# A fifth group of seven products in the values' second unit, and softmax's last scale on ScalarE

## The chip, the cores and the metric

The kernel runs on one core of one Trainium2 chip. The metric is the time of one execution on the device in microseconds, as the median of several runs. Everything is computed in float32 accuracy; there is one launch.

## The reference

One decoder layer on 256 tokens of width 2048. A combined projection feeds a state-space group of heads and an attention group; both outputs are concatenated, projected back and added to the input; a squared-ReLU MLP of width 8192 follows. RMSNorm stands before and after each half. What the change touches is the values' projection and the attention's softmax:

```python
proj = jnp.einsum('bsd,de->bse', u, w_in)
z, xbc, dt_raw, q, k, v = jnp.split(proj, IN_SPLITS, axis=-1)
...
s = jnp.where(mask[None, :, None], s, -jnp.inf)
m = jnp.max(s, axis=-1, keepdims=True)
p = jnp.exp(s - m)
den = jnp.sum(p, axis=-1)
o = jnp.einsum('bnqhk,bnkhd->bnqhd', p, vb) / jnp.swapaxes(den, 2, 3)[..., None]
```

There are three such branches (dilations 1, 4 and 16), weighted by their softmax denominators. The kernel folds them into one softmax, with the logarithm of the number of branches that see a key as the mask; the rows are divided by the sum before they are multiplied with the values.

## The kernel before

**Products in three.** TensorE multiplies in a reduced form of float32. So every factor is split in two: `hi`, the rounded value, written by ScalarE (L147), and `lo`, the rest, written by VectorE (L148). Each product is three matmuls: hi by hi, hi by lo, lo by hi. Weights are fetched as `raw` tiles of 256 x 512 (two blocks of 128 rows), split, and used as the moving side; the activations, split once, are the standing side. Tokens are two blocks of 128.

**Plain groups and groups of seven.** Most large projections are made in units: two blocks of 512 columns, walked over k, where one k is two 128-row blocks of weights. For one k there are two token blocks, two row blocks and two column blocks: eight products, 24 matmuls (`row_tile`, L331 to L333). In the form of Winograd's variant of Strassen's scheme (`seven`, L418 to L420) seven products of sums of blocks, 21 matmuls, do the same. They need sums of the weights' blocks (`add_in_line`, L252, three of 128x512 on VectorE), which are then split too: 3.5 tiles of 128x1024 instead of 2. They also need sums of the activations' blocks (`sums_of_acts`, L377 to L380 and a split of 128x512), which are kept per k in `room["sums"]` and used by every unit on the same activations. The sum of two row blocks of weights is made by GpSimd's DMA, which adds one block to the other in DRAM (`next_pair`, L279 and L280), four groups of seven ahead; SyncE then fetches that sum and the second block (L156 and L157) in place of one transfer (L161).

**What sets the order.** A scheduler orders each engine's instructions by the program's order and by priorities; splits, sums and combinations have a high one (`AHEAD`). `split_in_line` and `add_in_line` keep weights in one line. There are four raw tiles (`RAWS`) and five hi and lo tiles (`BUFS`). Which k come in which order, and which by seven, is a table per unit, the calls of `plan` (from L434 on); the same calls give the order of GpSimd's pairs.

**The stage.** Queries and keys of 4 heads at a time are computed with features in the partitions (`queries`, L485 and L488, blocks of `cT`, a ring of five tiles of 128 x 4 x 256) or by units with transposes behind. Around the change the program runs: queries of the last block; the values' second unit (`two_values(2, ...)`, with `room["sums"]` holding the sums of four k: 1, 3, 5, 6); keys of the last block; then the output projection. `own_places` takes two tiles of the ring as scratch for the unit. Meanwhile the heads' attention waits in a queue, from which each tile of a projection pumps a step; a unit drains it before its first group of seven. A step is: scores (L907, L908) for two heads; mask, row minimum of the negated scores (L915, VectorE), exponential with the row sum (L917, ScalarE), reciprocal (L919) and scale (L921, both VectorE); then transposes of the scaled rows (L929, TensorE) and their copies (L933, ScalarE); then the products with the values (L938, L939) and their split.

Of the kernel before, what the change touches and what calls it, by code (L numbers as in the profile page):

```python
# [11 lines left out]
F32R = mybir.dt.float32r  # L12
BF16 = mybir.dt.bfloat16
AF = mybir.ActivationFunctionType
ALU = mybir.AluOpType

P = 128
S = 256
# [21 lines left out]
KB = 2  # L40
# [13 lines left out]
V_SEVENS = (1, 3, 5, 6)  # L54
# [23 lines left out]
def hymba_layer(ctx: ExitStack, tc: tile.TileContext, x, norm_mix_pre, w_in, conv_w, conv_b, dt_bias, a_log,  # L78
                d_skip, ssm_norm_w, w_out, norm_mix_post, norm_mlp_pre, w_up, w_down, norm_mlp_post,
                consts, out):  # L80
    nc = tc.nc
# [31 lines left out]
    def part(k):  # L113
        if k < NK:
            return sh, sl, k
        i, r = divmod(k - NK, NK // 2)
        return (*att[i], r)
# [14 lines left out]
    def bank():  # L132
        return pacc.tile([P, NB], F32, name="acc")

    def psmall():
        return psm.tile([P, NB], F32, name="ps")
# [7 lines left out]
    def split(hi, lo, src, scale=None):  # L144

        if scale is None:
            return (nc.scalar.activation(hi, src, AF.Copy),  # L147
                    nc.vector.tensor_tensor(lo, src, hi.bitcast(F32), op=ALU.subtract))  # L148
        return (nc.scalar.activation(hi, src, AF.Copy, scale=scale),
                nc.vector.scalar_tensor_tensor(lo, src, scale, hi.bitcast(F32), op0=ALU.mult, op1=ALU.subtract))  # L150
# [27 lines left out]
    room = {}  # L178
# [77 lines left out]
    w_z, w_v, w_ups, w_downs = w_in[:, COL_Z:], w_in[:, COL_V:], [w_up[:, hf * 4096:] for hf in range(2)], [w_down, w_down[4096:]]  # L256
    orders = {}

    def order_of(ks, by_seven):
        return [(k, k in by_seven) for k in ks]  # L260

    def blocks_of(n):
        return n if isinstance(n, tuple) else (n * NB, (n + 1) * NB)

    def plan(name, src, n, order, by_seven):

        orders[name, n] = order_of(order, by_seven)
        pairs.extend((src, blocks_of(n), k) for k in order if k in by_seven)
# [167 lines left out]
    plan("qk", w_in, qk_blocks[1], (0, 2, 1, 4, 3, 5, 6), QK_SEVENS)  # L436
    plan("v", w_v, 0, range(7), V_SEVENS)
    plan("qk", w_in, qk_blocks[2], (0, 2, 1, 3, 4, 5, 6), QK_SEVENS)
    plan("v", w_v, 2, (0, 2, 1, 3, 4, 5, 6), V_SEVENS)
    plan("out", w_out, 0, (5, 7, 6, 9, 8, 11, 10, 13, 12), (6, 8, 9, 10, 12))  # L440
    plan("out", w_out, 2, (0, 6, 1, 9, 2, 12, 4, 3, 8, 5, 10, 7), (6, 9, 12, 4, 8, 10, 7))
    for hf in range(2):
# [8 lines left out]
    def unit(src, n, order, last, acc, more, combine, lag=0, at_end=(None, None), first=True, ending=None,  # L451
             ready=None, halves=None):


        cols = blocks_of(n)
        sevens = [k for k, by_seven in order if by_seven]
        for i, (k, by_seven) in enumerate(order):
            if i + 1 < len(order) and order[i + 1][1]:
                sums_of_acts(order[i + 1][0])
            if by_seven:  # L460
                if k == sevens[0]:
                    drain()
                    if ready:
                        ready()
                seven(src, *cols, k, acc, more, k == sevens[0], k == sevens[-1])
            else:
                for b in range(2):
                    row_tiles(src, cols[b], [k], acc[b::2], room["acts"], first and i == 0, False,
                              fetch=fetch_next)
            if k == sevens[-1]:  # L470
                combine(more)
        for b in range(2):
            if b and ending:
                ended.append(ending(cols[b], last, acc))
            else:
                row_tiles(src, cols[b], last, acc[b::2], room["acts"], False, True, lag if b else 0, at_end[b],
                          fetch=fetch_last if b else fetch_next, halves=halves if b else None)
# [173 lines left out]
    mp = mid.enter_context(tc.tile_pool(name="mp", bufs=1))  # L651
# [77 lines left out]
    def conv_block(c0, ft0, acc=None):  # L729

        first = acc
        acc = acc or gemm_features(w_in, c0)
        dst = mp.tile([P, 4, S], F32, name="cT", bufs=5)
        for b in range(2):
            added(dst[:, 2 * b:2 * b + 2], acc[2 * b:2 * b + 2])
        if first:
            waiting.append(first_conv(dst, ft0))
        else:
            conv(dst, ft0)
        return dst  # L740
# [28 lines left out]
    def own_places(tiles):  # L769

        own, total = tiles
        room["own"] = deque(own[:, t] for t in range(NT))
        room["sum"] = total
# [111 lines left out]
    for hb in range(2):  # L885
# [3 lines left out]
        cT = conv_block(COL_C + hb * NB, 24 + 4 * hb)  # L889
# [10 lines left out]
    def attention(ap, h, qT, kT, v):  # L900

        spans = ((slice(0, P), m0), (slice(P, 3 * P), m1))
        pair = []
        with tc.issue_after(product[0].ins), tc.issue_after(product[1].ins):
            for j in range(2):
                s = psmall()
                nc.tensor.matmul(s[:, 0:P], qT[:, j, 0:P], kT[:, j, 0:P], start=True, stop=True)  # L907
                nc.tensor.matmul(s[:, P:3 * P], qT[:, j, P:], kT[:, j], start=True, stop=True)  # L908
                pair.append(s)
        for j, s in enumerate(pair):  # L910
            sm = ap.tile([P, 3 * P], F32, name="sm", bufs=4)
            mx = ap.tile([P, 2], F32, name="mx", bufs=4)
            den = ap.tile([P, 2], F32, name="den", bufs=4)
            for t, (cs, mk) in enumerate(spans):
                nc.vector.tensor_tensor_reduce(sm[:, cs], s[:, cs], mk, op0=ALU.add, op1=ALU.min, scale=-1.0,  # L915
                                               scalar=3.0e38, accum_out=mx[:, t:t + 1])
                nc.scalar.activation(sm[:, cs], sm[:, cs], AF.Exp, bias=mx[:, t:t + 1], scale=-1.0,  # L917
                                     accum_out=den[:, t:t + 1])
            nc.vector.reciprocal(den, den)  # L919
            for t, (cs, mk) in enumerate(spans):  # L920
                nc.vector.tensor_scalar(sm[:, cs], sm[:, cs], den[:, t:t + 1], None, op0=ALU.mult)  # L921
            pair[j] = sm
        yield
        turned = []
        with tc.issue_after(product[0].ins), tc.issue_after(product[1].ins):
            for sm in pair:
                p = psmall()
                for b in range(3):
                    nc.tensor.transpose(p[:, b * P:(b + 1) * P], sm[:, b * P:(b + 1) * P], ident)  # L929
                turned.append(p)  # L930
        for j, p in enumerate(turned):
            pair[j] = ap.tile([P, 3 * P], F32, name="pT", bufs=4)
            nc.scalar.activation(pair[j], p[:, :3 * P], AF.Copy)  # L933
        yield
        o = psmall().rearrange("p (j s) -> p j s", j=2)
        with tc.issue_after(product[0].ins), tc.issue_after(product[1].ins):
            for j, pT in enumerate(pair):
                nc.tensor.matmul(o[:, j], v[:, 0, j], pT[:, :S], start=True, stop=False, skip_group_check=True)  # L938
                nc.tensor.matmul(o[:, j, P:], v[:, 1, j], pT[:, S:], start=False, stop=True, skip_group_check=True)  # L939
        d_h, d_l, i = part(NK + h)  # L940
        split(d_h[:, i:i + 2], d_l[:, i:i + 2], o)
# [56 lines left out]
    def two_values(vb, acc, more):  # L998

        values = []  # L1000

        def ready():
            values[:] = [mp.tile([P, NT, NB], F32, name="tk", bufs=3) for _ in range(2)]
            if not more:
                more.extend(f() for f in (psmall, bank, psmall, bank))

        def end(b):
            def at_end(t, a):
                with tc.high_priority(offset=AHEAD):
                    v = values[b][:, t]  # L1010
                    nc.vector.tensor_tensor(v, a, v, op=ALU.subtract if b else ALU.add)
                    nc.scalar.activation(v, v, AF.Copy, scale=rstd[:, t:t + 1])
            return at_end

        unit(w_v, vb, orders["v", vb], (7,), acc, more,
             lambda x: combine_new([[v[:, t] for t in range(NT)] for v in values], x), 0, (end(0), end(1)),
             ready=ready)
        return values
# [34 lines left out]
    heads((0, *qk[0], vs[0]), (1, *qk[1], vs[1]))  # L1053
    q3 = queries(COL_Q + 3 * NB, rbq, (1, 1, 0, 2, 1, 2, 2, 2))
    own_places([mp.tile([P, 4, S], F32, name="cT", bufs=5).rearrange("p (k f) s -> p k (f s)", k=KB) for _ in range(2)])
    vs += two_values(2, [bank() for _ in range(2 * NT)], [])
    heads((2, *qk[2], vs[2]))
    qk.append((q3, queries(COL_K + 3 * NB, rbc, (0, 0, 1, 1, 1, 1, 2, 2))))
# [498 lines left out]
```

## Time and profile before

| | before |
|---|---|
| runs | 1452.44, 1452.65, 1452.96 us |
| median | 1452.65 us |
| span of the profiled execution | 1451.4 us |
| TensorE busy | 1442.4 us, 99% |
| VectorE busy | 1300.4 us, 90% |
| ScalarE busy | 947.1 us, 65% |
| GpSimd busy | 162.3 us, 11% |
| mean granted clock | 0.999 |

The span is the time from the first to the last instruction of one profiled execution; what the runs take beside it is outside the program's instructions. Rows of a timeline give start, length, engine, line, operation and tiles; a bracket gives the idle time of the engine just before and what ended it. Rows that group instructions give the count, the busy time in us, the mean in ns, and behind the second bar the idle time before them. Matmuls overlap in the pipeline, so their starts, not their lengths, tell what one costs.

### The profile page before, as it was taken

The numbers are of one execution on the slowest core, as the hardware profiler recorded it, in microseconds if no ns is written. First come the engines' busy times: TensorE is split into PE (matmuls) and PEld (weight loads), VectorE is DVE, ScalarE is ACT, GpSimd is POOL, SyncE is SP. The second block draws the span as 40 slices with busy tenths as digits, with TensorE's granted clock in tenths as the row PEclk, the third lists the DMA queues.
The fourth block names the chain that finished last, engine by engine and source line by source line (L and its number), as shares of the span: only waits on it lengthen the run. The fifth ranks groups of instructions, "written<-read, shape, count | busy, mean of one in ns | idle before, by whom it ended". The sixth has DMA issues, their size and how long they took to land.

```text
span 1451.4 us, 20394 instructions
## 1 busy us (share of the span) xinstructions
PE 1442.4 (99%) x7042; PEld 1214.7 (84%) x7042; DVE 1300.4 (90%) x1881; ACT 947.1 (65%) x1351; POOL 162.3 (11%) x244
## 2 busy tenths in 40 slices
PE   9999999999999999999999999999999999999998
PEld 8888888888888888888888888888888888888886
DVE  7788888988999788689988999999889999999998
ACT  7577669665666666556657677656465776766664
POOL 0201110131111000010100011010111110101000
PEclk9999999999999999999999999999999999999999
DMA  8977656756898658588976798688888888788854
GB/s 267 272 219 222 189 175 187 239 170 195 231 253 248 196 127 244 173 270 257 280 225 217 210 311 240 203 221 251 249 255 279 255 245 247 210 293 265 248 179 160
DMA packets 172359, 332.97 MB, mean 229 GB/s; under 512 B 16048, under 2 KB 18976, under 8 KB 172256
## 3 DMA queue, kind: packets, MB, share of 16 engines
q1 hardware_dynamic: 144736, 272.37, 58.1%
q0 software_dynamic: 19648, 45.63, 15.7%
q10 hardware_dynamic: 7872, 13.68, 2.8%
q8 instruction: 55, 0.90, 0.3%
q14 instruction: 48, 0.39, 0.1%
HBM read 327.39 MB, written 49.84 MB: 260 GB/s over the span
## 4 chain that ended last, share of the span: by engine, by line
PE 76%; ACT 1%; DVE 1%; DMA 0%; issue 0%; ACTq 0%
PE acc L331 10%; PE acc L333 10%; PE acc L332 10%; PE acc L418 7%; PE acc L419 7%; PE acc L420 7%; PE acc L485 4%; PE ps L331 3%; PE ps L332 3%; PE ps L333 3%; PE ps L418 2%; PE ps L419 2%; PE ps L420 2%; PE acc L488 2%; PE acc L1463 1%; PE ps L938 0%
## 5 line engine op out<-in xcount | busy, mean ns | idle before, releaser
L148 DVE TENSOR_TENSOR lo<-raw,hi 128x1024 fp32r<-128x1024 f32 (+1 forms) x387 | 470.1, 1220 | 79.1 <-ACT hi L147 76.3
L147 ACT ACTIVATE hi<-raw 128x1024 fp32r<-128x1024 f32 (+1 forms) x387 | 404.2, 1050 | 204.2 <-PE acc L333 71.4
L485 PE MATMUL acc<-ua,hi 128*128 128x512 f32 x520 | 141.2, 401 | 0.1
L147 ACT ACTIVATE hi<-e 128x1024 fp32r<-128x1024 f32 x66 | 70.2, 1063 | 68.5 <-DVE e L252 62.7
L485 PEld LDWEIGHTS acc<-ua,hi 128*128 128x128 f32 x520 | 91.3, 189 | 14.2 <-ACT hi L147 0.2
L331 PE MATMUL acc<-hi,ua 128*128 128x512 f32 x228 | 90.6, 397 | 0.0
L332 PE MATMUL acc<-lo,ua 128*128 128x512 f32 x228 | 89.3, 392 | 0.0
L333 PE MATMUL acc<-hi,ua 128*128 128x512 f32 x228 | 89.2, 391 | 0.0
L331 PE MATMUL acc<-hi,sh 128*128 128x512 f32 x220 | 86.9, 395 | 0.0
L333 PE MATMUL acc<-hi,sl 128*128 128x512 f32 x220 | 85.8, 390 | 0.0
L332 PE MATMUL acc<-lo,sh 128*128 128x512 f32 x220 | 85.7, 390 | 0.0
L488 PEld LDWEIGHTS acc<-ua,lo 128*128 128x128 f32 x520 | 76.5, 190 | 8.9
L148 DVE TENSOR_TENSOR lo<-e,hi 128x1024 fp32r<-128x1024 f32 x66 | 80.5, 1220 | 0.0
L488 PE MATMUL acc<-ua,lo 128*128 128x256 f32 x520 | 78.8, 282 | 0.0
L419 PE MATMUL acc<-lo,ah 128*128 128x512 f32 x180 | 70.1, 390 | 0.0
L420 PE MATMUL acc<-hi,al 128*128 128x512 f32 x180 | 70.1, 390 | 0.0
L418 PE MATMUL acc<-hi,ah 128*128 128x512 f32 x180 | 70.1, 390 | 0.0
L485 PE MATMUL acc<-uc,hi 128*128 128x512 f32 x208 | 61.4, 405 | 0.0
L148 DVE TENSOR_TENSOR lo<-ha,hi 128x1024 fp32r<-128x1024 f32 x43 | 52.5, 1221 | 6.0 <-ACT hi L147 5.8
L147 ACT ACTIVATE hi<-ha 128x1024 fp32r<-128x1024 f32 x43 | 45.2, 1057 | 19.4 <-PE acc L333 12.4
L147 ACT ACTIVATE hi<-r 128x512 fp32r<-128x512 f32 x66 | 41.5, 629 | 20.8 <-PE acc L333 8.8
L418 PE MATMUL acc<-hi,ua 128*128 128x512 f32 x137 | 53.7, 392 | 0.0
(572 smaller groups left out, 3722.3 us busy)
## 6 DMA issues: line engine op xcount, KB each, us to landing
raw<-in_w_in_dram SPq DMA_DIRECT2D x154, 512.0 KB, 4.5
raw<-in_w_down_dram SPq DMA_DIRECT2D x69, 512.0 KB, 5.7
raw<-in_w_up_dram SPq DMA_DIRECT2D x65, 512.0 KB, 4.8
raw<-in_w_out_dram SPq DMA_DIRECT2D x38, 512.0 KB, 5.1
raw<-pair SPq DMA_DIRECT2D x57, 256.0 KB, 4.3
pair<-in_w_up_dram POOLq DMA_DIRECT2D x56, 256.0 KB, 5.4
pair<-in_w_down_dram POOLq DMA_DIRECT2D x52, 256.0 KB, 6.3
pair<-in_w_in_dram POOLq DMA_DIRECT2D x42, 256.0 KB, 5.5
```

The costliest lines, as they stand in the source:

```text
L147: return (nc.scalar.activation(hi, src, AF.Copy), nc.vector.tensor_tensor(lo, src, hi.bitcast(F32), op=ALU.subtract))
L148: nc.vector.tensor_tensor(lo, src, hi.bitcast(F32), op=ALU.subtract))
L331: nc.tensor.matmul(dst[:, cs], a_h[:, r, ts], hi[:, j, cs], start=begin and j == 0, stop=False)
L332: nc.tensor.matmul(dst[:, cs], a_h[:, r, ts], lo[:, j, cs], start=False, stop=False)
L333: product[t] = nc.tensor.matmul(dst[:, cs], a_l[:, r, ts], hi[:, j, cs], start=False, stop=end and j == KB - 1)
L418: nc.tensor.matmul(dst, a_h, hi[:, j], start=own and first, stop=False)
L419: nc.tensor.matmul(dst, a_h, lo[:, j], start=False, stop=False)
L420: nc.tensor.matmul(dst, a_l, hi[:, j], start=False, stop=own and last)
L485: nc.tensor.matmul(acc[f], hi[:, j, f * P:(f + 1) * P], u(k0 + j), start=k0 + j == 0, stop=False, skip_group_check=True)
L488: nc.tensor.matmul(acc[f][:, 0], lo[:, j, f * P:(f + 1) * P], u(k0 + j)[:, 0], start=False, stop=k0 + j == NK - 1, skip_group_check=True)
L1463: nc.tensor.transpose(p[:, f * P:(f + 1) * P], r[:, f * P:(f + 1) * P], ident)
```

## The change

The values' second unit takes k = 4 by seven products too: its table of sevens is written out as (1, 3, 4, 5, 6), where it was (1, 3, 5, 6), in the same order of k. The sums of k = 4 get a tile of the ring `cT` of their own, taken just before the unit; the keys' last block therefore takes the next tile of the ring. The last scale of the softmax, one instruction per head and token block, is an activation (a copy with a scale per partition) on ScalarE instead of a multiplication on VectorE.

```diff
-    plan("v", w_v, 2, (0, 2, 1, 3, 4, 5, 6), V_SEVENS)
+    plan("v", w_v, 2, (0, 2, 1, 3, 4, 5, 6), (1, 3, 4, 5, 6))
...
             nc.vector.reciprocal(den, den)
             for t, (cs, mk) in enumerate(spans):
-                nc.vector.tensor_scalar(sm[:, cs], sm[:, cs], den[:, t:t + 1], None, op0=ALU.mult)
+                nc.scalar.activation(sm[:, cs], sm[:, cs], AF.Copy, scale=den[:, t:t + 1])
             pair[j] = sm
...
     own_places([mp.tile([P, 4, S], F32, name="cT", bufs=5).rearrange("p (k f) s -> p k (f s)", k=KB) for _ in range(2)])
+    fifth = mp.tile([P, 4, S], F32R, name="cT", bufs=5)
+    room["sums"] += [fifth[:, i:i + KB] for i in (0, KB)]
     vs += two_values(2, [bank() for _ in range(2 * NT)], [])
```

## The prediction

> **What bounds the kernel now.** I read the page's busy shares and its chain first, then the engines' busy time in stretches of 25 us, then TensorE's and VectorE's timelines in the values' second unit.
>
> ```profile
> span 1451.4 us, 20394 instructions
> PE 1442.4 (99%) x7042; PEld 1214.7 (84%) x7042; DVE 1300.4 (90%) x1881; ACT 947.1 (65%) x1351; POOL 162.3 (11%) x244
> PE 76%; ACT 1%; DVE 1%; DMA 0%; issue 0%; ACTq 0%
> 500.00:525.00 25.00, 25.00 (x141) 21.42 (x140) 21.10 (x72) 17.53 (x49) 2.71 (x4) 1.00 0.54 127
> 525.00:550.00 25.00, 25.00 (x118) 20.83 (x117) 20.12 (x24) 15.11 (x18) 1.89 (x3) 1.00 0.59 170
> ```
>
> TensorE is never seen idle around the change (25.00 of 25), and the chain that ends last is TensorE's. So a matmul less is a gain, and anything that makes TensorE wait is a loss. VectorE has about 5 of 25 us to spare here, ScalarE 8 to 10. The profiled span is 1451.4 us; the timed runs' median is 1452.65, so 1.25 us lie around the span. The sum below is made on the span, and 1.25 is added at the end.
>
> How long a matmul really holds TensorE is read from starts, since neighbours overlap. The unit's fourth group (k = 4), in the plain form, and the two groups of seven after it:
>
> ```profile
> 540.71 0.39 PE L331 MATMUL acc<-hi,ua 128*128 128x512 f32 x1
> 546.15 0.39 PE L418 MATMUL ps<-hi,ub 128*128 128x512 f32 x1
> 550.91 0.39 PE L418 MATMUL ps<-hi,uc 128*128 128x512 f32 x1
> 555.67 0.39 PE L331 MATMUL acc<-hi,uc 128*128 128x512 f32 x1
> ```
>
> 24 matmuls take 546.15 - 540.71 = 5.44 us; 21 take 4.76 us, twice. One costs 0.227 us, not the 0.39 of its own row.
>
> VectorE over the same groups (columns: start, length, and in brackets the idle time before, with what ended it):
>
> ```profile
> 525.89 0.69 DVE L148 TENSOR_TENSOR lo<-cT,hi 128x512 fp32r<-128x512 f32 x1 [1.12 <-ACT hi L147]
> ...
> 529.71 1.23 DVE L148 TENSOR_TENSOR lo<-raw,hi 128x1024 fp32r<-128x1024 f32 x1 [1.79 <-ACT hi L147]
> ...
> 534.34 1.23 DVE L148 TENSOR_TENSOR lo<-cT,hi 128x1024 fp32r<-128x1024 f32 x1 [1.60 <-ACT hi L147]
> ...
> 537.30 2.58 DVE L148 TENSOR_TENSOR lo<-raw,hi 128x1024 fp32r<-128x1024 f32 x2
> 539.80 0.68 DVE L252 TENSOR_TENSOR cT<-raw 128x512 f32<-128x512 f32 x1
> 540.52 0.69 DVE L252 TENSOR_TENSOR cT<-cT,raw 128x512 f32<-128x512 f32 x1
> 541.12 1.22 DVE L148 TENSOR_TENSOR lo<-raw,hi 128x1024 fp32r<-128x1024 f32 x1
> 542.26 0.69 DVE L252 TENSOR_TENSOR cT<-cT,raw 128x512 f32<-128x512 f32 x1
> 542.86 1.22 DVE L148 TENSOR_TENSOR lo<-cT,hi 128x1024 fp32r<-128x1024 f32 x1
> 544.00 1.22 DVE L148 TENSOR_TENSOR lo<-raw,hi 128x1024 fp32r<-128x1024 f32 x1
> 545.13 0.69 DVE L148 TENSOR_TENSOR lo<-cT,hi 128x512 fp32r<-128x512 f32 x1
> 545.73 0.69 DVE L252 TENSOR_TENSOR cT<-raw 128x512 f32<-128x512 f32 x1
> ...
> 547.50 1.23 DVE L148 TENSOR_TENSOR lo<-raw,hi 128x1024 fp32r<-128x1024 f32 x1 [0.35 <-ACT hi L147]
> ```
>
> The rows 539.80 to 545.73 are one whole group of seven (k = 5): 5.93 us on VectorE, against 4.76 us on TensorE. The plain group (537.30 to 539.80) is 2.50 against 5.44. So VectorE falls behind by 1.17 us in every group of seven and wins 2.94 back in a plain one. That is the reading on which the forecast rests: the sevens are the cheap form for TensorE only while plain groups stand between them. Today the unit's order is plain, plain, 7, 7, plain, 7, 7, plain; with the change it is plain, plain, 7, 7, 7, 7, 7, plain.
>
> **The change part by part.** TensorE, k = 4: 24 matmuls become 21, 3 x 0.227 = **-0.68 us**. The remaining matmuls are the same.
>
> The four sums for k = 4 are new on VectorE; their nearest rows, from the view that groups by line and shape:
>
> ```profile
> L377 DVE TENSOR_TENSOR r<-ua 128x512 f32<-128x512 f32 x6 | 4.1, 686 | 0.0
> L378 DVE TENSOR_TENSOR r<-r 128x256 f32<-128x256 f32 x29 | 12.2, 422 | 0.5
> L379 DVE TENSOR_TENSOR r<-r 128x128 f32<-128x128 f32 x29 | 8.4, 289 | 0.4
> L380 DVE TENSOR_TENSOR r<-r 128x128 f32<-128x128 f32 x29 | 8.4, 289 | 0.4
> L148 DVE TENSOR_TENSOR lo<-r,hi 128x512 fp32r<-128x512 f32 x66 | 45.3, 687 | 0.7 <-ACT hi L147 0.7
> ```
>
> Together 2.37 us, less about 0.08 each for the overlap of neighbours (1.22 long, but 1.14 from 542.86 to 544.00): near 1.95. They stand ahead of the run, as VectorE's new order shows, among the rows of k = 1 and k = 3 (cT is here the scratch tile, raw the fetched weights, lo the rest after rounding, ps and al the attention's output):
>
> ```order
> L148 TENSOR_TENSOR lo<-cT,hi 128x1024
> L377 TENSOR_TENSOR cT<-ua 128x512
> L919 RECIPROCAL den<-den 128x2 x2
> ...
> L378 TENSOR_TENSOR cT<-cT 128x256
> L252 TENSOR_TENSOR cT<-cT,raw 128x512
> L379 TENSOR_TENSOR cT<-cT 128x128
> L380 TENSOR_TENSOR cT<-cT 128x128
> L148 TENSOR_TENSOR lo<-raw,hi 128x1024
> L148 TENSOR_TENSOR cT<-cT 128x512
> L252 TENSOR_TENSOR cT<-cT,raw 128x512
> L148 TENSOR_TENSOR al_4885<-ps,ah_4884 128x512 x2
> ```
>
> All of this is ahead of the row that is at 534.34 today, where VectorE idles 1.12, 1.79 and 1.60 us because ScalarE waits for TensorE to free a hi tile. I cost the sums at 0; without that cover they would cost up to 1.95.
>
> Behind that row no idle time is left but the 0.12 before 540.52 and 0.35 later, and there k = 4 is dearer. Before, from the tail of k = 3 on:
>
> ```order
> L148 TENSOR_TENSOR lo<-cT,hi 128x1024
> L148 TENSOR_TENSOR lo<-raw,hi 128x1024
> L148 TENSOR_TENSOR lo<-cT,hi 128x512
> L148 TENSOR_TENSOR lo<-raw,hi 128x1024 x2
> L252 TENSOR_TENSOR cT<-raw 128x512
> ```
>
> and with the change, the same place and the whole of k = 4:
>
> ```order
> L148 TENSOR_TENSOR lo<-cT,hi 128x1024
> L148 TENSOR_TENSOR lo<-raw,hi 128x1024
> L148 TENSOR_TENSOR lo<-cT,hi 128x512
> L252 TENSOR_TENSOR cT<-raw 128x512
> L252 TENSOR_TENSOR cT<-cT,raw 128x512
> L148 TENSOR_TENSOR lo<-raw,hi 128x1024
> L252 TENSOR_TENSOR cT<-cT,raw 128x512
> L148 TENSOR_TENSOR lo<-cT,hi 128x1024
> L148 TENSOR_TENSOR lo<-raw,hi 128x1024
> L148 TENSOR_TENSOR lo<-cT,hi 128x512
> ```
>
> The two lo rows of the plain group went, and seven rows came. So k = 4 starts on VectorE at 537.30, k = 5 at 543.23, k = 6 at 549.16. A group's first lo is done 2.54 after its start (541.12 + 1.22 - 539.80), its second 4.28 after. TensorE would start k = 4 at 540.71, k = 5 at 545.47, k = 6 at 550.23; the second matmul of a group (0.23 later) needs the first lo, the eighth (1.59) the second lo. k = 4: lo at 539.84, no wait. k = 5: first lo 545.77 against 545.70, wait 0.07; second lo 547.51 against 547.13, wait 0.38. k = 6: first lo 551.70 against 550.91 (0.45 late already), wait 0.79; second lo 553.44 against 553.06, wait 0.38. The third and fourth come in time. Sum of waits **+1.62 us**. Bounds: 0, if VectorE is relieved by more than I count, and 3 x 1.17 + 1.95 = 5.5, if in the last three groups the tiles ready ahead, and for the sums the idle time, are worth nothing. I stay with the row-by-row value.
>
> The softmax scale leaves VectorE: 32 instructions. Its rows, and the nearest ScalarE rows with a scale per partition:
>
> ```profile
> L921 DVE TENSOR_SCALAR sm<-sm,den 128x256 f32<-128x256 f32 x16 | 5.6, 348 | 0.0
> L921 DVE TENSOR_SCALAR sm<-sm,den 128x128 f32<-128x128 f32 x16 | 4.6, 286 | 0.4
> L1407 ACT ACTIVATE dg<-ident,rff 128x128 f32<-128x128 f32 x1 | 0.4, 401 | 0.2 <-DVE rff L1401 0.2
> L1012 ACT ACTIVATE tk<-tk,rstd 128x512 f32<-128x512 f32 x8 | 5.3, 707 | 0.0
> ACT sm L917 <- DVE mx L915: 11.0, 10, 1.7
> PEld ps L929 <- DVE mx L915: 0.4, 2, 0.2
> PEld ps L929 <- ACT pT L933: 0.3, 1, 0.3
> ```
>
> VectorE gives up 10.2 us; ScalarE takes 16 x 0.401 + 16 x 0.503 (a third of the way from 401 to 707) = 14.5, on top of 32.6 busy of 50 us in the two stretches above. The scale now waits on ScalarE for VectorE's reciprocal, and a weight tile's hi can be queued behind it:
>
> ```order
> L917 ACTIVATE sm,den<-sm,mx 128x128
> L921 ACTIVATE sm<-sm,den 128x128
> L147 ACTIVATE hi<-raw 128x1024
> L921 ACTIVATE sm<-sm,den 128x256
> L917 ACTIVATE sm,den<-sm,mx 128x256
> ```
>
> Here hi (L147), which stood behind four exponentials (L917), stands between two scales, the first of which can start only when the reciprocal is there; behind it TensorE's next weights wait. ScalarE already waits 11.0 us for VectorE in this chain without TensorE stopping; TensorE's transposes (L929), which need the scaled rows, waited 0.7 us in all. Bounds: -0.7, when those waits go, and 16 heads x (0.904 - 0.634 for the two scales of a head) = +4.3, when every transpose is late by the dearer scale. I take **0**, near the rows of the transposes' waits, since the order puts other matmuls between scale and transpose.
>
> ScalarE's own share of the new group (1.5 tiles of 1.06 and one of 0.63) is 2.2 us of the same slack: 0. Transfers: SyncE issues three pieces in place of two for k = 4, the bytes into raw are equal; GpSimd issues one more pair (two transfers), asked for four groups of seven ahead. The keys' last block moves to the place of the third queries, which the scores leave long before it is written: 0. Behind these rows every engine's order is as it was, so what TensorE loses here it keeps. **Sum: -0.68 + 1.62 + 0 = +0.94**; span 1452.3, time **1453.6 us**.
>
> **The rivals.** *All hidden.* VectorE, relieved of the scales, runs the sums early and is far enough ahead: no wait, -0.68, 1452.0. For it: the idle time ahead of 534.34. Against it: that idle time is a wait for free hi tiles (BUFS is 5, a group of seven uses four), so work cannot be put there beyond five tiles.
>
> *Weights land late (slower).*
>
> ```profile
> DMA to landing us min/median/max: 3.5/4.5/11.3
> SPq L156 <- DVE lo L148: 19.0, 6, 4.6
> ```
>
> With four raw tiles and two used per group, a fetch goes out when VectorE has split the tile two groups back, and must land within 2 x 5.93 - 5.42 = 6.4 us (5.42: from 539.80 to the third lo's end). The median is 4.5, so it decides only from 6.4 on. At 7.9 (half-way to the maximum) in three groups it adds 3 x 1.5 = 4.5: 1458.1. For it: the last three groups fall where transfers share the engines with the pairs. Against it: the bytes are the same.
>
> *The scale is late on ScalarE (slower).* +4.3, so 1457.9; it decides if the transposes' waits of 0.7 us in all become one of 0.27 for every head. The Trainium skill ("ScalarE: Activation LUTs", section "Rules for kernel authors") speaks for it: it lists a plain multiply as work for VectorE, not ScalarE. By its section "What ACT_TABLE_LOAD costs" an activation with one pointer operand takes about 280 ns + 0.833 ns per column, an estimate of 387 and 493 ns here and 14.1 us for the 32; the trace's 401 ns agrees.
>
> **How the numbers follow.** A measurement of this kernel tells about 0.2% (2.9 us) from no change. Forecast, a small loss (its own range 1452.7 to 1455.3): 0.60. All hidden: 0.22. Late weights: 0.06. Late scale: 0.08. A gain over 0.2%: 0.02, since 0.68 + 0.7 us is all that the rows offer. What is left, 0.02, is a place I have not seen, such as the keys' last block waiting for its new tile. Slower by over 0.2% holds the two slow rivals and the forecast's edge, 0.15; within 0.2% 0.83; faster 0.02. The range, 1451.4 to 1456.6, leaves out most of the two slow rivals.
>
> **What would show it.** In the profile after: TensorE's rows in k = 5 and k = 6 longer than 0.39 or waiting for VectorE's lo (L148), 1 to 2 us in all; no bracketed idle time on VectorE from the tail of k = 3 to the end of k = 6; the first matmul of k = 5 4.76 us behind that of k = 4; L921 on ScalarE near 0.40 and 0.50; transposes' waits under 1 us. I am wrong if TensorE runs five groups in 23.8 us without a wait, or if L929 waits by several us.

## The result and the profile after

| | before | after |
|---|---|---|
| median of 19 runs each, side by side | 1452.96 us | 1455.42 us |
| lowest, highest | 1452.44, 1454.87 | 1454.72, 1457.19 |
| ratio of the times, 95% interval | | 1.0016 (1.0010 to 1.0022) |
| span of the profiled execution | 1451.4 us | 1454.1 us |

The changed kernel is slower by 2.5 us, 0.16%. The interval lies above 1, so the loss is real, though it is smaller than the 0.2% that the prediction took for the least that can be told from no change. The time is inside the prediction's range; the forecast was 1453.6 us, so it was 1.8 us too low. 0.3 of that is the kernel before, which has 1452.96 in these runs and had 1452.65 when the forecast was made.

The page of the kernel after, and its engines' busy time in the two stretches shown of before and in the one behind them:

```profile
span 1454.1 us, 20412 instructions
PE 1444.2 (99%) x7039; PEld 1213.8 (83%) x7039; DVE 1297.5 (89%) x1859; ACT 958.6 (66%) x1386; POOL 163.7 (11%) x246
PE 74%; DVE 2%; ACT 2%; DMA 0%; issue 0%; ACTq 0%; DVEq 0%
...
500.00:525.00 25.00, 25.00 (x140) 20.69 (x139) 17.66 (x56) 20.94 (x60) 2.71 (x4) 1.00 0.52 128
525.00:550.00 25.00, 24.94 (x116) 20.01 (x115) 20.83 (x29) 16.50 (x25) 3.26 (x5) 1.00 0.56 150
550.00:575.00 25.00, 24.09 (x119) 19.75 (x118) 21.47 (x32) 15.78 (x23) 0.81 (x1) 1.00 0.77 237
```

Three matmuls went (7042 to 7039), and TensorE's share of the chain fell from 76 to 74%: VectorE and ScalarE now stand in it with 2% each. Between 500 and 525 the scale's move is plain to see: VectorE fell from 21.10 to 17.66, ScalarE rose from 17.53 to 20.94. Between 550 and 575 TensorE is short of 25 us by 0.91, where before it was not:

```profile
550.00:575.00 25.00, 25.00 (x131) 21.53 (x130) 20.83 (x32) 15.76 (x26) 0.81 (x1) 1.00 0.84 244
```

TensorE in the unit, rows of k = 4 to k = 6 (start, length, line; idle time in brackets) of the kernel after:

```profile
541.61 0.39 PE L418 MATMUL ps<-hi,ua 128*128 128x512 f32 x1
...
546.37 0.39 PE L418 MATMUL ps<-hi,ub 128*128 128x512 f32 x1
546.59 0.39 PE L418 MATMUL acc<-hi,ub 128*128 128x512 f32 x1
547.04 0.50 PE L419 MATMUL ps<-lo,ub 128*128 128x512 f32 x1
547.38 0.40 PE L420 MATMUL ps<-hi,ub 128*128 128x512 f32 x1
...
551.52 0.39 PE L418 MATMUL ps<-hi,uc 128*128 128x512 f32 x1
551.75 0.39 PE L418 MATMUL acc<-hi,uc 128*128 128x512 f32 x1
553.02 0.50 PE L418 MATMUL acc<-hi,ah 128*128 128x512 f32 x1 [0.88 <-ACT hi L147]
553.37 0.40 PE L419 MATMUL ps<-lo,uc 128*128 128x512 f32 x1
```

k = 5 starts 546.37 - 541.61 = 4.76 us behind k = 4, as the prediction said. Then two stalls: 0.45 between the starts 546.59 and 547.04, where 0.227 is normal, and 1.27 between 551.75 and 553.02. Behind each the next start is 0.11 late (547.38 - 547.04 = 0.34). By these starts the waits of k = 5 come to 0.34 us and those of k = 6 to 1.16; the prediction had 0.45 and 1.17. VectorE and ScalarE over the same stretch:

```profile
535.63 1.23 DVE L148 TENSOR_TENSOR lo<-cT,hi 128x1024 fp32r<-128x1024 f32 x1 [1.55 <-ACT hi L147]
...
538.50 0.69 DVE L252 TENSOR_TENSOR cT<-raw 128x512 f32<-128x512 f32 x1
...
544.45 0.68 DVE L252 TENSOR_TENSOR cT<-raw 128x512 f32<-128x512 f32 x1
...
550.38 0.69 DVE L252 TENSOR_TENSOR cT<-raw 128x512 f32<-128x512 f32 x1
551.10 0.69 DVE L252 TENSOR_TENSOR cT<-cT,raw 128x512 f32<-128x512 f32 x1
```

```profile
551.91 1.06 ACT L147 ACTIVATE hi<-cT 128x1024 fp32r<-128x1024 f32 x1 [2.46 <-DVE cT L252]
```

VectorE's groups start 5.95 and 5.93 us apart, without idle time. The long stall of TensorE is put down to ScalarE's hi, but this hi itself waited 2.46 us for VectorE's second sum of k = 6 (551.10), which was queued behind the last rows of k = 5. So the name in TensorE's bracket is the last link, not the cause.

The rest lies outside the groups of seven. To see where, I take from each trace the start of four matmuls that all kernels have, as a difference to the kernel before, less the difference that TensorE's 101st matmul (at 18.9 us) already has. That last one was between 0.63 early and 0.31 late in single executions, and stays the same within 0.05 us up to 465 us, so it has nothing to do with the edits. The cells of the two spread orders are empty where that group stands in another place:

| | median, us (before, same chip) | ratio, 95% interval | 101st matmul | first group of seven | transposes of the keys' block, first | scores in the output projection |
|---|---|---|---|---|---|---|
| before | | | 0 | 0 (530.96) | 0 (577.84) | 0 (593.20) |
| after | 1455.42 (1452.96) | 1.0016 (1.0010 to 1.0022) | +0.11 | +0.63 | +2.03 | +2.57 |
| fifth group alone | 1454.43 (1452.95) | 1.0010 (1.0001 to 1.0018) | -0.15 | +0.30 | +1.40 | +1.38 |
| scale alone | 1454.06 (1452.95) | 1.0008 (1.0000 to 1.0017) | -0.63 | +0.53 | +0.44 | +1.47 |
| four groups in a row | 1453.63 (1452.95) | 1.0006 (0.9997 to 1.0015) | +0.15 | +0.36 | +0.70 | +0.41 |
| five groups, spread | 1456.59 (1452.95) | 1.0027 (1.0016 to 1.0037) | -0.21 | | +3.08 | +3.08 |
| scale alone, exponentials first | 1453.58 (1453.02) | 1.0001 (0.9992 to 1.0010) | +0.06 | +0.31 | +0.16 | -0.13 |
| fifth group, one lo per group left out | 1452.36 (1453.02) | 0.9997 (0.9988 to 1.0005) | -0.31 | +0.05 | -0.67 | -0.87 |
| fifth group, a sum on GpSimd | 1458.41 (1453.02) | 1.0033 (1.0021 to 1.0046) | +0.31 | +1.09 | +5.14 | +4.86 |
| spread, attention pumped earlier | 1456.14 (1453.02) | 1.0023 (1.0014 to 1.0032) | -0.09 | | +2.91 | +2.61 |
| after, exponentials first | 1455.18 (1453.07) | 1.0016 (1.0007 to 1.0025) | +0.10 | +0.31 | +1.34 | +1.89 |

After: +0.63 ahead of the unit, +1.40 from there to the keys' transposes, +0.54 at them; behind that, up to the last matmul, no run's shift changes by more than 0.14 us. Each row is one profiled execution. The last column's values agree with the medians within 0.7 us; three of the ten ratios have 1 inside their interval, one has it at its edge, and the intervals of the two parts overlap with each other, so the places in the trace carry the argument, not the medians.

### The profile page after: what moved, and what is told of

Its sections match the earlier page's. It is cut to its first block, busy times and chain, and to the rows that moved or that the text cites. A ratio compares the mean times of both kernels' runs of the same rounds, so it can differ in the third digit from the quotient of the medians.

```text
span 1454.1 us, 20412 instructions
## 1 busy us (share of the span) xinstructions
PE 1444.2 (99%) x7039; PEld 1213.8 (83%) x7039; DVE 1297.5 (89%) x1859; ACT 958.6 (66%) x1386; POOL 163.7 (11%) x246
## 4 chain that ended last, share of the span: by engine, by line
PE 74%; DVE 2%; ACT 2%; DMA 0%; issue 0%; ACTq 0%; DVEq 0%
PE acc L331 10%; PE acc L333 10%; PE acc L332 10%; PE acc L418 6%; PE acc L419 6%; PE acc L420 6%; PE acc L485 3%; PE ps L333 3%; PE ps L331 3%; PE ps L332 3%; PE ps L418 2%; PE ps L419 2%; PE ps L420 2%; PE acc L488 2%; DVE lo L148 1%; PE acc L1465 1%
## 5 line engine op out<-in xcount | busy, mean ns | idle before, releaser
L148 DVE TENSOR_TENSOR lo<-raw,hi 128x1024 fp32r<-128x1024 f32 (+1 forms) x387 | 469.5, 1218 | 81.9 <-ACT hi L147 78.8
L485 PE MATMUL acc<-ua,hi 128*128 128x512 f32 x520 | 141.0, 400 | 0.0
L485 PEld LDWEIGHTS acc<-ua,hi 128*128 128x128 f32 x520 | 91.5, 189 | 14.6 <-ACT hi L147 0.4
L331 PE MATMUL acc<-hi,ua 128*128 128x512 f32 x220 | 87.4, 397 | 0.0
L333 PE MATMUL acc<-hi,ua 128*128 128x512 f32 x220 | 86.3, 392 | 0.0
L332 PE MATMUL acc<-lo,ua 128*128 128x512 f32 x220 | 86.1, 391 | 0.0
L148 DVE TENSOR_TENSOR lo<-e,hi 128x1024 fp32r<-128x1024 f32 x66 | 80.4, 1218 | 0.0
L485 PE MATMUL acc<-uc,hi 128*128 128x512 f32 x208 | 61.5, 405 | 0.0
L148 DVE TENSOR_TENSOR lo<-ha,hi 128x1024 fp32r<-128x1024 f32 x43 | 52.5, 1220 | 5.9 <-ACT hi L147 5.7
L418 PE MATMUL acc<-hi,ua 128*128 128x512 f32 x139 | 54.5, 392 | 0.0
```

The source lines that it names most:

```text
L331: nc.tensor.matmul(dst[:, cs], a_h[:, r, ts], hi[:, j, cs], start=begin and j == 0, stop=False)
L332: nc.tensor.matmul(dst[:, cs], a_h[:, r, ts], lo[:, j, cs], start=False, stop=False)
L333: product[t] = nc.tensor.matmul(dst[:, cs], a_l[:, r, ts], hi[:, j, cs], start=False, stop=end and j == KB - 1)
L418: nc.tensor.matmul(dst, a_h, hi[:, j], start=own and first, stop=False)
L485: nc.tensor.matmul(acc[f], hi[:, j, f * P:(f + 1) * P], u(k0 + j), start=k0 + j == 0, stop=False, skip_group_check=True)
```

## The experiments

**The two parts apart.** First the fifth group with the scale left on VectorE:

```diff
-                nc.scalar.activation(sm[:, cs], sm[:, cs], AF.Copy, scale=den[:, t:t + 1])
+                nc.vector.tensor_scalar(sm[:, cs], sm[:, cs], den[:, t:t + 1], None, op0=ALU.mult)
```

> The fifth group of seven alone; softmax's last scale stays on VectorE. The changed kernel is 2.46 us above the one before by the medians (2.7 by the spans), of which its trace puts 0.7 ahead of the unit, 1.5 in it and 0.5 in the keys' last block. Theory 1, two separate prices (VectorE cannot follow five groups of seven in a row: -0.68 for three matmuls, about +2.2 of waits; the scale on ScalarE: +1.2 ahead of the unit and behind it): only the unit's part is left, +1.5 on the kernel before, within 0.4; TensorE's wait in front of k = 6 of about 1 us is still there. Rival A, the scale carries all of it (ScalarE's hi come late because scales stand between them): the waits in the unit go, -0.7 to 0. Rival B, the fifth group carries all of it, the parts ahead and behind too (its tile of the ring, its sums among the attention's work): +2.5.

Then the scale on ScalarE alone, with the unit as before:

```diff
-    plan("v", w_v, 2, (0, 2, 1, 3, 4, 5, 6), (1, 3, 4, 5, 6))
+    plan("v", w_v, 2, (0, 2, 1, 3, 4, 5, 6), V_SEVENS)
...
-    fifth = mp.tile([P, 4, S], F32R, name="cT", bufs=5)
-    room["sums"] += [fifth[:, i:i + KB] for i in (0, KB)]
```

> The scale on ScalarE alone; the unit keeps four groups of seven. Theory 1: +1.2 on the kernel before (0.7 before the unit's first group of seven, 0.5 at the keys' transposes), none of it inside the groups of seven. Rival A: +2.5 to +3.2, waits for ScalarE's hi inside the unit. Rival B: 0 within 0.4.

Measured: +1.38 and +1.47, together 2.85 against 2.57 for both. With the fifth group alone the waits in the unit are there (1.06 ahead of k = 6, 1.57 in all) and TensorE's transposes in the keys' block cost nothing. With the scale alone the unit is untouched (0.53 ahead of it, 0.44 behind it), and 1.0 us is lost at the second transposes of the keys' block. So neither rival holds: it is two prices at two places (and a smaller third where the two parts meet, shown further down). The shares differ from what was expected in two things: the fifth group alone already loses 0.30 ahead of the unit, and the scale alone loses 1.0 at the transposes, where 0.5 was expected. In the changed kernel the scale adds 2.57 - 1.38 = 1.19, less than alone.

**What the scale costs.** TensorE and ScalarE around the second transposes of the keys' block, scale alone:

```profile
581.62 0.55 PE L929 MATMUL ps<-ident,sm 128*128 128x128 f32 x3
582.69 0.55 PE L929 MATMUL ps<-ident,sm 128*128 128x128 f32 x3 [0.52 <-ACT pT L933]
```

```profile
578.97 1.04 ACT L147 ACTIVATE hi<-raw 128x1024 fp32r<-128x1024 f32 x1
579.92 0.79 ACT L921 ACTIVATE sm<-sm,den 128x128 f32<-128x128 f32 x2
580.61 0.50 ACT L917 ACTIVATE sm<-sm,mx 128x256 f32<-128x256 f32 x1
...
581.10 0.47 ACT L933 ACTIVATE pT<-ps 128x384 f32<-128x384 f32 x1
581.47 0.79 ACT L921 ACTIVATE sm<-sm,den 128x128 f32<-128x128 f32 x2
582.16 0.47 ACT L933 ACTIVATE pT<-ps 128x384 f32<-128x384 f32 x1
```

The last exponential of the pair (L917, 580.61) stands behind a weight tile's hi and two scales of the other head. Its own scale (581.47) comes only after the reciprocal, and the copy (L933, 582.16) that frees the place of the next transposes comes behind that scale. TensorE waits for that copy. To see whether it is the place in the line or the price of the scale, both heads' exponentials were written ahead of the scales, with the same instructions:

```diff
             nc.vector.reciprocal(den, den)
-            for t, (cs, mk) in enumerate(spans):
-                nc.scalar.activation(sm[:, cs], sm[:, cs], AF.Copy, scale=den[:, t:t + 1])
+            pair[j] = sm, den
+        for j, (sm, den) in enumerate(pair):
+            for t, (cs, mk) in enumerate(spans):
+                nc.scalar.activation(sm[:, cs], sm[:, cs], AF.Copy, scale=den[:, t:t + 1])
             pair[j] = sm
```

> The scale on ScalarE alone, as in the scale-only run, but both heads' four exponentials are written ahead of the four scales, so that no exponential stands behind a scale. In the scale-only run TensorE lost 1.5 us from its first loads to the output projection (+0.9 in the span, with a start 0.6 earlier): 0.5 ahead of the unit, 1.0 at the second transposes of the keys' last block, where an exponential stood on ScalarE behind a scale that waited for VectorE's reciprocal. Theory: what costs is the scale's place in ScalarE's line; then the 1.0 shrinks to 0.3 or less. Rival: what costs is that the scale is dearer and the copies of the transposes share an engine with it; then the 1.0 stays. The part ahead of the unit may go either way, since TensorE's order changes there.

The 1.0 is gone (the last two columns of the table: +0.16, -0.13). The same place in this run, ScalarE and TensorE:

```profile
577.98 0.49 ACT L917 ACTIVATE sm<-sm,mx 128x256 f32<-128x256 f32 x1
...
578.48 1.04 ACT L147 ACTIVATE hi<-raw 128x1024 fp32r<-128x1024 f32 x1
579.42 1.48 ACT L921 ACTIVATE sm<-sm,den 128x128 f32<-128x128 f32 x4
580.81 0.84 ACT L933 ACTIVATE pT<-ps 128x384 f32<-128x384 f32 x2
```

```profile
581.51 0.82 PE L929 MATMUL ps<-ident,sm 128*128 128x128 f32 x6
```

All exponentials are done ahead of the hi, four scales run in one go, the copies follow, and the six transposes start together. The scales are as dear as before (0.40 and 0.50 for the two shapes) and cost nothing by the output projection, where the 0.31 lost ahead of the unit has come back: the price is the place in ScalarE's line. The same edit on the changed kernel:

> The changed kernel (fifth group, scale on ScalarE) with the four exponentials of a pair of heads written ahead of the four scales. If the two parts of the change simply add and the scale's price is its place in ScalarE's line, what is left is the fifth group's part: as the run of the fifth group alone, +1.3 in the span on the kernel before (less or more by the start, which differs by up to 0.6 between executions), and some 1 us less than the changed kernel; at the keys' second transposes no wait over 0.2; in the unit still the wait of about 1 us ahead of the last group. Rival: the relief of VectorE by the scales is worth something to the unit once the scales no longer hold ScalarE up: then the unit's waits fall well under 1.5.

Here it helped only by half (0.68 of the scale's 1.19): ahead of the unit 0.31 in place of 0.63, from there to the keys' transposes 1.03 in place of 1.40, but at these still 0.55. The order that came out is another one. ScalarE in this run:

```profile
580.11 1.05 ACT L147 ACTIVATE hi<-raw 128x1024 fp32r<-128x1024 f32 x1
581.06 0.50 ACT L917 ACTIVATE sm<-sm,mx 128x256 f32<-128x256 f32 x1
...
582.62 0.79 ACT L921 ACTIVATE sm<-sm,den 128x128 f32<-128x128 f32 x2
583.31 0.48 ACT L933 ACTIVATE pT<-ps 128x384 f32<-128x384 f32 x1
```

The hi still stands ahead of the last exponential, and behind it the same chain follows: reciprocal, scale, copy, transposes. So my expectation for the place was wrong, while the chain that loses the time is the same. The rival of that run, that VectorE's relief helps the unit, does not show: 1.03 from the first group of seven to the keys' transposes, 1.10 with the scale on VectorE, and the stall ahead of k = 6 is still 1.04 us.

**What the fifth group costs.** Four groups as before, but in a row:

```diff
-    plan("v", w_v, 2, (0, 2, 1, 3, 4, 5, 6), V_SEVENS)
+    plan("v", w_v, 2, (0, 2, 1, 3, 4, 5, 6), (1, 3, 4, 5))
```

(with the tile for the fourth sums as in the change, scale on VectorE.)

> Four groups of seven as before, but next to each other (k = 1, 3, 4, 5), and the plain group k = 6 behind them instead of between; scale on VectorE. No matmul is saved. Theory 1: by the changed kernel's trace the first three groups in a row cost nothing and the fourth (k = 5) waits about 0.35, the fifth would wait about 1.2; so +0.2 to +0.5. Rival C, weights that land late (each group of seven needs two fetched tiles and the fetches cannot follow): the waits in k = 5 end on a transfer, +0.5 or more. If the position of the plain group is without effect: 0.

Measured +0.41. In the fourth group TensorE waits 0.29 and 0.11, near the waits of k = 5 in the changed kernel (0.34), so the wait is where it was expected. That the total fits too is luck: 0.36 more is lost ahead of the unit, and 0.29 comes back behind it. Next, VectorE's pace itself: in the five groups the lo of the second weight block is left out (TensorE multiplies by hi a second time in its place, so the values are not the layer's), 1.14 us per group less on VectorE:

```diff
-            hl_b = parts()
-            split_in_line(*hl_b, raw_b)
+            hi_b = wp.tile([P, KB, NB], F32R, name="hi", bufs=BUFS)
+            with in_line():
+                line["act"] = nc.scalar.activation(hi_b, raw_b, AF.Copy)
+            hl_b = hi_b, hi_b
```

> The fifth group alone (scale on VectorE), and in this unit's five groups the lo of the fetched second block (raw_b) is not computed; its products use hi in its place, so this output is not the layer's. TensorE's and ScalarE's work stays; VectorE has 1.23 us less per group, 4.8 instead of 5.93, level with TensorE's 4.76. Theory (VectorE's pace in the row of groups makes the waits of 1.57 us seen with the fifth group alone): the waits in the unit fall under 0.4, and the time is 1.2 to 1.5 below that of the fifth group alone, so at or just under the kernel before (-0.5 to +0.2). Rival (ScalarE: the profile names its hi as what ended the longest wait; or transfers): the wait of 1.06 ahead of the last group stays, +1.4.

The engines' busy time in one stretch, with the fifth group alone:

```profile
530.00:555.00 25.00, 23.97 (x106) 19.06 (x105) 23.04 (x28) 15.64 (x20) 3.52 (x5) 1.00 0.65 173
```

and with that lo left out:

```profile
530.00:555.00 25.00, 25.00 (x113) 20.52 (x112) 21.61 (x26) 17.79 (x21) 2.91 (x5) 1.00 0.81 216
```

TensorE's idle time is gone, both stalls with it, though ScalarE and the transfers do all their work. From the first group of seven to the keys' transposes it is now -0.72, the three matmuls (-0.68). The lo that is left out is not the tile that either stall waited for, so the waits are VectorE's pace over groups in a row. In all the run is at -0.87, below the expected -0.5 to +0.2, since the 0.30 ahead of the unit is gone as well (0.05). Three matmuls are also all that a fifth group saves here, 0.05%.

**Ways around it.** A plain group between the groups of seven, scale on VectorE:

```diff
-    plan("v", w_v, 2, (0, 2, 1, 3, 4, 5, 6), (1, 3, 4, 5, 6))
+    plan("v", w_v, 2, (0, 1, 3, 2, 4, 5, 6), (1, 3, 4, 5, 6))
```

> Five groups of seven, but the plain group k = 2 stands between them: order 0, 1, 3, 2, 4, 5, 6; scale on VectorE. 21 matmuls less in all groups as in the changed kernel. Theory 1: a plain group gives VectorE 2.94 us back, so that the last three groups follow without a wait: -0.7, less what the earlier drain of the attention costs (a plain group less of 5.44 us between the attention's steps, unknown, 0 to +1). Rival B: +2.5 still, since the fifth group's tile and sums are the same. If the waits come from the number of groups of seven and not from their order, as in the first run of this call.

("The first run" is the fifth group alone. The matmuls of this run are three less than before, 7039, as in the changed kernel.) The last three groups are 553.50 - 543.98 = 2 x 4.76 us apart:

```profile
543.98 0.39 PE L418 MATMUL ps<-hi,ua 128*128 128x512 f32 x1
...
553.50 0.39 PE L418 MATMUL ps<-hi,uc 128*128 128x512 f32 x1
```

so the plain group does what the theory says, and yet the run is the second slowest, +3.08. The first two groups of seven now run one plain group earlier, among the attention's steps:

```profile
510.00:535.00 25.00, 23.63 (x115) 18.16 (x114) 22.47 (x55) 15.69 (x36) 0.55 (x1) 1.00 0.36 101
535.00:560.00 25.00, 25.00 (x112) 20.17 (x112) 23.45 (x30) 15.93 (x19) 3.53 (x5) 1.00 0.77 199
```

TensorE loses 1.4 us in the first stretch, where VectorE makes softmax, the sums of k = 4 and the weights' sums at once (22.47 of 25). More steps of the attention were then put into the third queries:

```diff
-    q3 = queries(COL_Q + 3 * NB, rbq, (1, 1, 0, 2, 1, 2, 2, 2))
+    q3 = queries(COL_Q + 3 * NB, rbq, (1, 2, 1, 2, 2, 2, 2, 2))
```

> The spread order (0, 1, 3, 2, 4, 5, 6) with five groups of seven and the scale on VectorE, and the third queries pump the waiting attention more often (1, 2, 1, 2, 2, 2, 2, 2 steps instead of 1, 1, 0, 2, 1, 2, 2, 2). The spread run had no wait over 0.11 in its last three groups of seven, but 2.8 us of waits in its first two, among which the attention's transposes and products now stood. Theory: these 2.8 are the attention that is no longer done ahead of the groups of seven; with more steps ahead, in the queries, they mostly go: -0.7 to +0.5. Rival (the first two groups themselves come too early for VectorE, which makes their sums while it still does softmax): +1.5 or more.

+2.61: by the number the rival's case. But the theory was not put to the test: nine of the second pair's twelve transposes still start at 525.94 or later, behind the first group of seven (522.09), so the extra steps did not get the attention out of the way. With the order of the changed kernel the first group starts only behind the last of the attention's products. The plain group ahead of the groups of seven is thus not only a rest for VectorE, it is also where the attention ends; neither of the two orders tried gives both, and which of the two costs the time in the spread order stays open. Last, one of the three weight sums on GpSimd:

```diff
-            add_in_line(t4, e[:, 1], raw_a[:, 1])
+            nc.gpsimd.tensor_tensor(t4, e[:, 1], raw_a[:, 1], op=ALU.add)
```

> The fifth group alone (scale on VectorE), and in this unit the third sum of weight blocks of each group (128x512) is made by GpSimd instead of VectorE. VectorE needs 5.33 instead of 5.93 per group, so it falls behind by 0.57 instead of 1.17 per group. Theory (VectorE's pace): the waits of 1.57 fall to 0 to 0.5, time -0.5 to +0.3 against the kernel before. Rival (GpSimd's line: the sum stands behind a pair's transfers that GpSimd waits for, or GpSimd's own sum is so long that the group's last tile comes late, or slows VectorE's rows): new waits ahead of the last three matmuls of each group, +1 or more.

+4.86, the slowest of all: the rival's case, by its last clause. GpSimd's and VectorE's rows at one such sum (the line is L400 in this kernel):

```profile
547.06 1.89 POOL L400 TENSOR_TENSOR cT<-cT,raw 128x512 f32<-128x512 f32 x1
```

```profile
546.57 1.22 DVE L148 TENSOR_TENSOR lo<-raw,hi 128x1024 fp32r<-128x1024 f32 x1
547.87 2.17 DVE L148 TENSOR_TENSOR lo<-cT,hi 128x1024 fp32r<-128x1024 f32 x1
549.96 1.21 DVE L148 TENSOR_TENSOR lo<-raw,hi 128x1024 fp32r<-128x1024 f32 x1
```

The lo that runs while GpSimd adds takes 2.17 in place of 1.21 us. VectorE was spared one sum of 0.6 and lost 0.96. In two other groups the row beside GpSimd's took 2.32.

## Why the prediction was right or wrong

The likeliest case came, a small loss under 0.2%, with the right sign. Two things about it were not right. A loss of 0.16% can be told from none, by nineteen runs on each side. And the loss is more than twice the sum's +0.94: the time stands 0.1 us above that case's own range (1452.7 to 1455.3). What the sum put at nothing came to 1.8 us (2.57 less -0.72 and 1.50); the full range held that because it is wide, not because the sum had the places. By its own steps:

- *A group of seven holds VectorE 5.93 and TensorE 4.76 us.* Right: 5.95, 5.93 and 4.76 in the profile after. Leaving out 1.14 us of VectorE's work per group took the waits away.
- *-0.68 for three matmuls.* Right: -0.72 where nothing else interferes.
- *Waits of +1.62 in k = 5 and k = 6.* Right in sum: 1.50 in the changed kernel, 1.57 with the fifth group alone. Wrong in which instruction waits: I let the second and eighth matmul of a group wait for a lo (L148). TensorE's order has more of the hi products ahead, and the long stall is one for the sums' hi, behind VectorE's sum (L252). The lag per group was right; that the sum of the waits fits within 0.12 is in part luck.
- *The sums of k = 4 at 0, in VectorE's idle time.* The row on VectorE stands where I said,

```profile
L377 DVE TENSOR_TENSOR cT<-ua x1: 687/687/687, 521.3 to 521.3; 128x512 f32<-128x512 f32 x1
```

  ahead of the row at 535.63. But 0.30 is lost ahead of the unit with the fifth group alone, and 0.36 with four in a row. In both, the second pair's twelve transposes (L929) stand in four places among TensorE's plain products (with the fifth group alone from 521.46, 523.53, 525.09 and 525.88), where before they stood in three (521.59, 522.85 and 525.03). With one lo per group left out, the same sums are made, the transposes stand in three places, and only 0.05 is lost. So the loss goes with the order on TensorE and not with VectorE's time for the sums; the order was not varied by itself. I had looked for idle time on VectorE only.
- *The scale at 0, "since the order puts other matmuls between scale and transpose".* This is the step that failed. It cost 1.47 alone, and 1.19 in the changed kernel: 0.54 at the keys' transposes, about 0.3 ahead of the unit (0.63, of which 0.30 is there without it) and about 0.3 between the two (1.40, of which 1.10 is there without it; the next point shows where). The durations were right: forecast 0.401 and 0.503, measured

```profile
L921 ACT ACTIVATE sm<-sm,den 128x128 f32<-128x128 f32 x16 | 6.3, 392 | 1.5 <-DVE den L919 1.5
L921 ACT ACTIVATE sm<-sm,den 128x256 f32<-128x256 f32 x16 | 7.9, 495 | 0.0
```

  This also agrees with the estimate of 387 and 493 ns from the Trainium skill ("ScalarE: Activation LUTs", section "What ACT_TABLE_LOAD costs"). What I missed is not the scale's own wait of 1.5 us but what is queued behind it: the copies of the transposes (L933) stand in the same line. The prediction named hi as the tile that could be late and left L933 out. The bounds (-0.7 to +4.3) held it. The rival that priced every transpose dearer is refuted with it: with the exponentials first the same dear scales cost nothing.
- *Missing from the sum:* about 0.6 between the last group of seven and the keys' transposes (1.40 = -0.72 + 1.50 + the rest). Half of it is one more wait. The keys' first product (L485) needs a weight tile's hi, and its weight load waits 0.44 us for it:

```profile
560.50 0.39 PE L333 MATMUL acc<-hi,uc 128*128 128x512 f32 x1
560.91 0.50 PE L485 MATMUL acc<-ua,hi 128*128 128x512 f32 x1
561.24 0.40 PE L332 MATMUL acc<-lo,uc 128*128 128x512 f32 x1
```

```profile
560.90 0.19 PEld L485 LDWEIGHTS acc<-ua,hi 128*128 128x128 f32 x1 [0.44 <-ACT hi L147]
```

  The starts are 0.41 and 0.33 apart, where 0.227 is normal: 0.29 us. With the fifth group alone the same product stands between the same two lines and starts 0.23 behind and 0.23 ahead of its neighbours. With the scale alone nothing is lost between these two marks either (0.53, then 0.44). So this wait takes both parts of the change; that ScalarE's hi itself began late there (559.79, 2.97 us behind its row before, and released by a product of the last plain group) is in the trace, but why was not tested. The other half, 0.25 with the fifth group alone (1.10 = -0.72 + 1.57 + 0.25), stays open. In both runs the keys' scores (L907, L908) stand in three places instead of two, and starts come up to 0.2 us late behind each of these.
- *Weights land late; the unit free of waits.* Neither happened: no wait of TensorE in the unit ends on a transfer, and it does wait.

What would show it, the prediction said, are waits of the transposes under 1 us. By the weight loads (PEld), from which it took its 0.7, they are 2.1 us; the last row is the matmuls' own wait, part of the same stall:

```profile
PEld ps L929 <- ACT pT L933: 1.1, 3, 0.6
PEld ps L929 <- ACT sm L921: 0.8, 3, 0.3
PEld ps L929 <- ACT sm L917: 0.2, 1, 0.2
PE ps L929 <- ACT pT L933: 0.3, 1, 0.3
```

1.1 of them end on the copy, which was 0.3 before.

## What to carry to other kernels

Before a cheaper form is used once more, compare what one group takes on the engine that is full with what it takes on the engine that feeds it: if the feeder is slower, its lag adds up from group to group, and what counts is how many stand in a row, not how many there are. When an instruction moves to an engine with spare time, its length may cost nothing; list what stands behind it in that engine's line, above all what frees a place for the full engine, and what it waits for itself. And a wait is put down to the last link: go on from the engine named to what that one waited for.

## What was not expected of the hardware

- A GpSimd addition of 128x512 beside VectorE's two-operand rows: VectorE's row of 1.21 us took 2.17 to 2.32, and GpSimd's own five took between 1.28 and 2.04. The Trainium skill ("SBUF — State Buffer", section "Who interferes with whom") says that a VectorE instruction with two inputs from this memory contends with a GpSimd instruction that reads it; it calls the ports that the two share an exclusive lock, and says that issue order decides who blocks. The rows agree: VectorE's row of 547.87 stands still until GpSimd ends at 547.06 + 1.89 = 548.95, and then needs 1.09 up to 550.04, near its usual 1.2. GpSimd's row in turn began while VectorE's row of 546.57 ran, and of its 1.89 us 1.16 lie behind that row's end. The expectation of that run had slower VectorE rows only as one of three rivals, without a size.
- TensorE's 101st matmul lies up to 0.63 us earlier or 0.31 later than in the kernel before from one profiled execution to the next, though no edit stands ahead of it, and the shift stays up to where the edits begin. The first loads have a part in it: before, TensorE waits 0.43 us for a tile of the input at 7.9 us, and with the scale alone, the earliest, it does not. At effects of 1 us, spans of single executions have to be compared from there.
- Behind each of TensorE's two stalls in the unit, the next matmul starts 0.11 us late again, whether the stall was 0.22 or 1.05 us.
